# Loading later, more scratch buffers and spread spatial products in the projection phase of a hybrid decoder step

## The chip, the cores and the metric

The kernel runs on one core of one Trainium2 chip. The metric is the device time of one execution in microseconds (us), the median of several runs. The engines are called PE (TensorE, the matmuls), PEld (its weight loads, which overlap with PE), DVE (VectorE), ACT (ScalarE), POOL (GpSimd) and SP (SyncE, which here issues almost all DMAs).

## The reference

One layer of a hybrid decoder, for a prompt of 2048 tokens (16 blocks of 128 rows) and for 64 rows of a sample batch (8 sequences of 8 tokens, with 1024 cached tokens each). Cut to what matters here:

```python
def project(x, pos, norm_g, w_in, qn_g, kn_g, ln_g, ln_b, w_s, b_s):
    h = rmsnorm(x, norm_g)
    z = h @ w_in                                   # 1024 -> 3656 columns
    q, k, v, qi, ki, wi, ga, u, vm, gm = jnp.split(z, offs, axis=-1)
    ...                                            # RMSNorm and partial rotary on q, k; rotary on qi, ki
    vn = layernorm(jax.nn.gelu(vm), ln_g, ln_b)
    s = chunk_spatial_gate(vn, w_s, b_s)           # per group g: tril(w_s[g]) @ vn of each 128-row chunk
    gm_out = jax.nn.gelu(u) * s * jax.nn.silu(gm)

def indexer_scores(qi, wi, ki):
    dots = jnp.einsum('bthd,bld->bthl', qi, ki)
    return jnp.einsum('bth,bthl->btl', wi, jax.nn.relu(dots))

# per block of 128 queries: the 256 best causal keys by indexer score (top-k),
# attention over those keys only, output times silu(ga); then concat with gm_out,
# output projection, residual, and a gated per-layer embedding.
```

The sample rows do the same with keys from a paged cache, which are found through `page_table`.

## The kernel before

A class `Builder` writes the whole program: `phase_a` projects, scores and selects; `phase_b` attends; `phase_c` does the output side. The change lies in `phase_a` alone.

`phase_a` takes the blocks in three rounds (`ROUNDS`): blocks 0 to 4 and the sample block (SB), then 5 to 10, then 11 to 15. In each round it goes over 14 column chunks of `w_in` (`CH`), in the order x1 (indexer key, head weights and half of the indexer queries, 328 columns), x2 (the other half of the queries), vm0, vm1, k, v, u0, u1, gm0, gm1, q0, q1, ga0, ga1 (256 columns each). A chunk's weights are split into a rounded high part `whi` and a remainder `wlo`. In round 0, `load_w` (L265) brings them as eight `raw` tiles (L281) from a pool of six buffers, POOL or ACT writes `whi` (L287 on POOL), DVE writes `wlo` (L288), and `keep_w` (L291, its DMAs L293) writes both back to DRAM, so that rounds 1 and 2 load them ready. There are two `whi` and two `wlo` tiles: the weights of the next chunk are asked for at the start of the current one.

`proj` (L305) does a block's matmuls: `whi` and `wlo` with `hhi` (L318, L319), then `whi` with `hlo` (L321); for the sample block L311, L312 and an evacuation through `vt` (L314 on ACT, L315 on DVE). Their result `z` has two PSUM buffers. `hhi` and `hlo` are the transposed, split inputs (PE L249, ACT L123, DVE L124). `post` (L346) treats `z` by the chunk's name. For x1 it copies the indexer key to `kin` (ACT L357, a tile with two buffers), rotates it (DVE L132 to L135), sends it to the output (SP L361, `idx_k_prompt<-kin`) and transposes it into `ki_stack` (PE L365, ACT L367, DVE L368); the queries go as `qn` to the DRAM scratch `s_qi` (L378, L381). For vm1 the LayerNorm is `vst` (L423 to L425), then `vn` times and plus `lng` on POOL (L429, L430). `spatial` (L331) is the mixing product of one group for all blocks of the round: PE L337 (prompt blocks) and L342 (sample), out through ACT L338 and L343 into the `vn` tile, with two `tp` PSUM buffers shared with all transposes. In round 0 the eight groups are called from chunk k's block 3 on and through chunk v.

Beside the projections runs the indexer. After each block's `post` the function `pump` is called with a budget and draws steps from generators: `idx` (the queries are loaded by `load_qi` L652 and transposed L666, then dots on PE L681/L682, relu on ACT L684, weighted sum on DVE L686), `sample_idx` for the sample block (its keys come by indirect DMA on POOL, L695, with the row numbers `prow` that `page_rows` computes on DVE, L189 and L190), and `topk` (a search for the threshold, ACT L822 with short DVE steps, then full-width DVE passes). After round 2 the last part of `phase_a` computes the gMLP half of the output projection (`gm` products: PE L560 transposes, L572, L573, L576 matmuls) while the last top-ks run, and prepares the keys of phase B (PE L1014, ACT L1016, DVE L1017).

The order in which the code is written is a priority; a scheduler at build time fixes the order of instructions on each engine and of DMAs on SP. On the chip each engine then works strictly in that order.

Of the kernel before, what the change touches and what calls it, by code (L numbers as in the profile page):

```python
# [9 lines left out]
F32 = mybir.dt.float32  # L10
# [13 lines left out]
SB = 16  # L24
# [17 lines left out]
FILL_AT = 4  # L42
LAG_SM = 4
# [67 lines left out]
class Builder:  # L111
# [85 lines left out]
    def phase_a(self, eb):  # L197
        tc, nc, I, O = self.tc, self.nc, self.I, self.O
        with ExitStack() as es:
# [13 lines left out]
            rp = pool("a_raw", 6)  # L213
# [131 lines left out]
            def post(name, b, z):  # L345
# [3 lines left out]
                if name == "x1":  # L349
                    w = z[:, 64:72]  # L350
                    if b == SB:
                        nc.vector.tensor_scalar(self.absw[:P, b], w, rs, (8 * 64) ** -0.5, op0=OP.mult, op1=OP.mult)
                    else:
                        nc.scalar.activation(self.absw[:P, b], w, AF.Abs, scale=self.rs2[:P, b:b + 1])
                        nc.scalar.activation(self.sgn[:P, b], w, AF.Sign)
                    kin2 = wk.tile([128, 2, 64], F32, name="kin")[:P]
                    nc.scalar.activation(kin2, z[:, None, 0:64].to_broadcast([P, 2, 64]), AF.Copy, scale=rs)  # L357
                    self.rope(nc.vector, kin2, rt, 2, wk, P)
                    kin = kin2[:, 0]
                    dst = O["idx_k_sample"].rearrange("o a t d -> (o a t) d") if b == SB else O["idx_k_prompt"][0, 0, b * 128:(b + 1) * 128]  # L360
                    nc.sync.dma_start(dst, kin)  # L361

                    def ki_t():
                        ps = self.tp.tile([128, 4, 128], F32, name="tp")
                        nc.tensor.transpose(ps[:, 0, :P], kin2.rearrange("p a d -> p (a d)"), ident[:P, :P])  # L365
                        kst = self.ki[:, b, :P]
                        nc.scalar.activation(kst, ps[:, 0, :P], AF.Copy)  # L367
                        nc.vector.tensor_tensor(kst[64:128], ps[64:128, 0, :P], kst[64:128].bitcast(F32), OP.subtract)  # L368

                    later.append(ki_t)  # L370
# [76 lines left out]
            primed, active = [], [None]  # L447
# [3 lines left out]
            def pump(budget):  # L451
                credit[0] = min(credit[0], 0.0) + budget
                while credit[0] > 0 and (blocks_due or primed or dots or tops):
                    if not primed and blocks_due and not (dots and active[0] == SB):
# [3 lines left out]
                    if not dots and primed and len(tops) < 2:  # L458
                        active[0], g = primed.pop()
                        dots.append(g)  # L460
                    turn[0] ^= 1
                    l = (dots, tops)[turn[0]]
                    if l:
                        try:
                            v = next(l[0])
                            if isinstance(v, tuple):
                                tops.append(self.topk(*v))
                                v = 0
                            credit[0] -= v
                        except StopIteration:  # L470
# [16 lines left out]
            for si, (r, c) in enumerate(seq):  # L487
# [9 lines left out]
                nxt = load_w(seq[si + 1][1], seq[si + 1][0]) if si + 1 < len(seq) else None  # L497
                if si == 0:
# [4 lines left out]
                    lng = ac.tile([128, 2, 512], F32, name="lng")  # L503
                    nc.sync.dma_start(lng[:, 0], bcast(I["ln_v_g"], 512))
                    nc.sync.dma_start(lng[:, 1], bcast(I["ln_v_b"], 512))
# [10 lines left out]
                    self.io8 = io8  # L516
                    self.cnew = tk.tile([64, 64], F32, name="cnew")
# [3 lines left out]
                if not nxt:  # L521
                    ws = [load_out(0)]
                for j, b in enumerate(blocks):
                    z = proj(cur, b)
                    for f in later:
                        f()
                    later.clear()
                    post(name, b, z)
                    n, s = 2 * len(blocks) - 2, {"k": j - 2, "v": len(blocks) - 2 + j}.get(name, -1)
                    if s >= 0:  # L530
                        for g in range(8 * s // n, 8 * (s + 1) // n):
                            spatial(blocks, g)
# [1047 lines left out]
```

## Time and profile before

| | us |
|---|---|
| median of 3 runs | 1902.33 |
| the three runs | 1901.91, 1902.33, 1904.38 |
| the profiled execution | 1904.02 |
| its span (first to last instruction) | 1902.2 |
| PE busy in the span | 1835.5 (96%) |
| DVE busy | 1244.3 (65%) |
| ACT busy | 1018.8 (54%) |
| POOL busy | 631.2 (33%) |
| DMA traffic | 261.54 MB, mean 137 GB/s |

PE's share is the first number to read: what PE does not work, or works at half clock, is all that an edit of order can win in the stretches in which it is the bound. A row of waits reads: engine, tile and line that waited, the engine, tile and line waited for, the total in us, how often, and the longest.

### The profile page before, as it was taken

Reading aid. Unit: us, or ns where it says so; the run is one execution under the profiler, and the core shown is the slowest. Engines: PE = TensorE matmul, PEld = TensorE weight load, DVE = VectorE, ACT = ScalarE, POOL = GpSimd, SP = SyncE. Lnnn points to the kernel's source line nnn. Section 1 sums busy time; section 2 is a strip of 40 time slices with the busy share of each in tenths; the row PEclk is TensorE's granted clock in tenths of the full one; section 3 lists DMA queues with packets and bytes.
Section 4 is the critical chain, followed back from the end, with each engine's and each line's share of the span. In section 5 each row is a group of like instructions: output and inputs, shape, how many; then the busy total and the mean of one; then the engine's idle time right before and its main releaser. Section 6 shows DMA issues by size and latency. Waiting matters only on the chain. (4 is left out here: it accounts for less than half of the span.)

```text
span 1902.2 us, 33981 instructions
## 1 busy us (share of the span) xinstructions
PE 1835.5 (96%) x11974; PEld 1602.0 (84%) x11974; DVE 1244.3 (65%) x3631; ACT 1018.8 (54%) x1909; POOL 631.2 (33%) x950
## 2 busy tenths in 40 slices
PE   7989998999999999999989899999999999999998
PEld 6889978999999999999867678777787777888887
DVE  4497655458778638778752789888998765223321
ACT  4245434346666636667654788877888653122221
POOL 4483463324003324004403443232221374222221
PEclk9989999999999999999999899999999999999999
DMA  8655656544445564454463432233220373222211
GB/s 285 200 163 180 207 188 210 186 131 147 127 155 169 202 188 141 151 164 166 139 206 130 134 102 87 66 100 95 67 67 23 98 246 130 75 96 99 98 36 45
DMA packets 243807, 261.54 MB, mean 137 GB/s; under 512 B 83176, under 2 KB 209840, under 8 KB 243248
## 3 DMA queue, kind: packets, MB, share of 16 engines
q1 hardware_dynamic: 237744, 240.45, 40.0%
q0 software_dynamic: 5888, 18.88, 3.3%
q8 instruction: 95, 1.56, 0.3%
q14 instruction: 80, 0.66, 0.1%
HBM read 171.90 MB, written 87.37 MB: 136 GB/s over the span
## 5 line engine op out<-in xcount | busy, mean ns | idle before, releaser
L318 PE MATMUL z<-whi,hhi 128*128 128x256 f32 (+1 forms) x1792 | 461.2, 292 | 11.3 <-ACT qn L392 3.9
L319 PE MATMUL z<-wlo,hhi 128*128 128x256 f32 (+1 forms) x1792 | 453.1, 287 | 0.2 <-DVE wlo L288 0.2
L318 PEld LDWEIGHTS z<-whi,hhi 128*128 128x128 f32 x1792 | 341.0, 190 | 22.1 <-ACT qn L392 4.3
L319 PEld LDWEIGHTS z<-wlo,hhi 128*128 128x128 f32 x1792 | 340.9, 190 | 5.7 <-DVE wlo L288 1.5
L321 PE MATMUL z<-whi,hlo 128*128 128x256 f32 (+1 forms) x1792 | 264.4, 286 | 0.0
L321 PEld LDWEIGHTS z<-whi,hlo 128*128 128x128 f32 x1792 | 238.4, 190 | 2.4
L686 DVE SCALAR_TENSOR_TENSOR big<-dots,sgn,big 128x1024 f32<-128x1024 f32 (+7 forms) x176 | 179.2, 1018 | 62.3 <-ACT dots L684 58.2
L124 DVE TENSOR_TENSOR b_pt<-b_tp,b_pt 128x512 fp32r<-128x512 f32 (+1 forms) x288 | 183.3, 655 | 11.8 <-ACT b_pt L123 10.5
L684 ACT ACTIVATE dots<-dots 128x1024 f32<-128x1024 f32 (+7 forms) x176 | 140.7, 802 | 93.0 <-PE dots L682 88.1
L1148 PE MATMUL b_o<-b_pt,Vst 128*128 128x512 f32 x544 | 183.7, 423 | 0.9 <-DVE b_pt L124 0.8
L123 ACT ACTIVATE b_pt<-b_tp 128x512 fp32r<-128x512 f32 (+1 forms) x288 | 155.5, 577 | 49.4 <-PE b_tp L1131 44.2
L1131 PE MATMUL b_tp<-mats,b_sm 128*128 128x128 f32 x1088 | 171.9, 275 | 3.1 <-DVE b_pt L124 1.8
L822 ACT ACTIVATE bfw<-big,tk 128x384 bf16<-128x384 f32 (+14 forms) x105 | 136.4, 1299 | 52.6 <-DVE tk L842 38.1
L1105 ACT ACTIVATE b_sm<-b_sm,b_st 128x128 f32<-128x128 f32 (+15 forms) x128 | 154.8, 1210 | 15.7 <-DVE b_st L1098 14.6
L1131 PEld LDWEIGHTS b_tp<-mats,b_sm 128*128 128x128 f32 x1088 | 131.5, 141 | 34.9 <-ACT b_sm L1105 4.9
L1096 PE MATMUL b_s<-Kst,b_qh 128*128 128x512 f32 (+3 forms) x320 | 139.5, 439 | 6.9 <-DVE b_st L1098 4.3
L1098 DVE CUSTOM_DVE_ANT_0 b_sm<-b_s,b_mask,b_st 128x512 f32<-128x512 f32 (+3 forms) x192 | 123.9, 646 | 24.8 <-PE b_s L1097 17.3
L1097 PE MATMUL b_s<-Kst,b_ql 128*128 128x512 f32 (+3 forms) x320 | 117.4, 369 | 0.0
L681 PE MATMUL dots<-ki_stack,qih 128*128 128x512 f32 (+3 forms) x304 | 112.7, 372 | 1.6 <-DVE big L686 1.6
L1464 PE MATMUL c_mm<-c_l_w_ple_gate,c_mh 128*128 128x512 f32 x272 | 107.1, 394 | 2.6 <-DVE c_l_w_ple_gate L1417 2.6
L682 PE MATMUL dots<-ki_stack,qil 128*128 128x512 f32 (+3 forms) x304 | 109.6, 369 | 0.0
L1463 PE MATMUL c_mm<-c_h_w_ple_gate,c_mh 128*128 128x512 f32 x272 | 109.3, 402 | 0.0
(351 smaller groups left out, 3758.4 us busy)
## 6 DMA issues: line engine op xcount, KB each, us to landing
whi<-s_wh SPq DMA_DIRECT2D x52, 512.0 KB
wlo<-s_wl SPq DMA_DIRECT2D x52, 512.0 KB
raw<-w_in SPq DMA_DIRECT2D x112, 128.0 KB
s_wh<-whi SPq DMA_DIRECT2D x13, 1024.0 KB
s_wl<-wlo SPq DMA_DIRECT2D x13, 1024.0 KB
s_r<-hlo SPq DMA_DIRECT2D x32, 256.0 KB
b_qr<-s_q SPq DMA_DIRECT2D x32, 256.0 KB
c_r<-s_r SPq DMA_DIRECT2D x16, 512.0 KB
```

The lines of the kernel that those rows point to most:

```text
L123: nc.scalar.activation(hi, src, AF.Copy)
L124: nc.vector.tensor_tensor(lo, src, hi.bitcast(F32), OP.subtract)
L318: nc.tensor.matmul(z, lhsT=hh[:, k], rhs=wh[:, k, :n], start=(k == 0), stop=False)
L319: nc.tensor.matmul(z, lhsT=hh[:, k], rhs=wl[:, k, :n], start=False, stop=False)
L321: nc.tensor.matmul(z, lhsT=hl[:, k], rhs=wh[:, k, :n], start=False, stop=(k == 7))
L684: nc.scalar.activation(r, r, AF.Relu)
L686: nc.vector.scalar_tensor_tensor(a, r, self.sgn[:, b, h:h + 1], a, op0=OP.mult, op1=OP.add)
L822: nc.scalar.activation(junk, acc[:P], AF.Sign, bias=cur[:, 0:1], accum_out=cur[:, 1:2])
L1096: nc.tensor.matmul(ps, lhsT=qh[:, h], rhs=rhs, start=True, stop=False)
L1105: nc.scalar.activation(part, part, AF.Exp, bias=stt[:, h, c:c + 1], scale=-1.0, accum_out=stt[:, h, 4 + e:5 + e])
L1131: nc.tensor.transpose(ps[:, k, r], sm2[r][:, (k0 + k) * 128:(k0 + k) * 128 + 128], ident)
L1148: nc.tensor.matmul(o.rearrange("p a b -> p (a b)"), lhsT=Vst[:, kb, g].rearrange("p a d -> p (a d)"), rhs=pt[:, k].rearrange("p a b -> p ( ...
```

## The change

Six things change, all in `phase_a`. The `kin` tile has four buffers (KIN) where it had the two of its pool, and the `raw` pool five where it had six. `pump` asks for the queries of the next indexer block only after four dots steps of the current one, and, when no dots are left, puts the top-k that has just done a step at the end of the list, so that two top-ks would go in turns. The constants that were loaded in the first chunk (x1) are divided: the small matrices, `guess`, the query and key norms and two index rows go to chunk x2, the LayerNorm rows `lng`, `cnew` and `page_rows` to chunk vm0. The weights of the next chunk are asked for after the first block's projection (round 0) or the second's (rounds 1 and 2). The spatial products are called one per block: four on the last blocks of chunk v and four on the first blocks of u0.

```diff
@@ -40,6 +40,7 @@
 FILL = 128
 PV_YIELD = 1
 FILL_AT = 4
+KIN = 4
 LAG_SM = 4
 LEAD = 2
 SPS = 0
@@ -210,7 +211,7 @@
             self.wk2 = right("a_wk2", 1)
             hp = pool("a_h", 6)
             wp = pool("a_w", 2)
-            rp = pool("a_raw", 6)
+            rp = pool("a_raw", 5)
             xp = ei.enter_context(tc.tile_pool(name="a_x", bufs=2, reuse_waits="tile"))
             self.big = big
             self.dp = pool("a_dots", 2, space=PSUM)
@@ -353,7 +354,7 @@
                     else:
                         nc.scalar.activation(self.absw[:P, b], w, AF.Abs, scale=self.rs2[:P, b:b + 1])
                         nc.scalar.activation(self.sgn[:P, b], w, AF.Sign)
-                    kin2 = wk.tile([128, 2, 64], F32, name="kin")[:P]
+                    kin2 = wk.tile([128, 2, 64], F32, name="kin", bufs=KIN)[:P]
                     nc.scalar.activation(kin2, z[:, None, 0:64].to_broadcast([P, 2, 64]), AF.Copy, scale=rs)
                     self.rope(nc.vector, kin2, rt, 2, wk, P)
                     kin = kin2[:, 0]
@@ -444,29 +445,33 @@
             self.idx_rate = 0
             blocks_due, dots, tops = [], [], []
 
-            primed, active = [], [None]
+            primed, active, steps = [], [None], [0]
 
             credit, turn = [0.0], [0]
 
             def pump(budget):
                 credit[0] = min(credit[0], 0.0) + budget
                 while credit[0] > 0 and (blocks_due or primed or dots or tops):
-                    if not primed and blocks_due and not (dots and active[0] == SB):
+                    if not primed and blocks_due and not (dots and (active[0] == SB or steps[0] < 4)):
                         b = blocks_due.pop(0)
                         primed.append((b, self.sample_idx() if b == SB else self.idx(b)))
                         next(primed[0][1])
                     if not dots and primed and len(tops) < 2:
                         active[0], g = primed.pop()
+                        steps[0] = 0
                         dots.append(g)
                     turn[0] ^= 1
                     l = (dots, tops)[turn[0]]
                     if l:
                         try:
                             v = next(l[0])
+                            steps[0] += l is dots
                             if isinstance(v, tuple):
                                 tops.append(self.topk(*v))
                                 v = 0
                             credit[0] -= v
+                            if l is tops and not (dots or primed or blocks_due):
+                                tops.append(tops.pop(0))
                         except StopIteration:
                             l.pop(0)
 
@@ -494,15 +499,11 @@
                         vslot[b] = (t, j)
                 if si == 2:
                     self.gmlp_weights(ac)
-                nxt = load_w(seq[si + 1][1], seq[si + 1][0]) if si + 1 < len(seq) else None
-                if si == 0:
+                if si == 1:
                     self.more_mats()
                     guess = tk.tile([128, 17, 3], F32, name="guess")
                     nc.sync.dma_start(guess, I["c_guess"])
                     self.guess = guess
-                    lng = ac.tile([128, 2, 512], F32, name="lng")
-                    nc.sync.dma_start(lng[:, 0], bcast(I["ln_v_g"], 512))
-                    nc.sync.dma_start(lng[:, 1], bcast(I["ln_v_b"], 512))
                     self.qkg = qkg = ac.tile([128, 2, 64], F32, name="qkg")
                     nc.sync.dma_start(qkg[:, 0], bcast(I["q_norm_g"], 64))
                     nc.sync.dma_start(qkg[:, 1], bcast(I["k_norm_g"], 64))
@@ -514,22 +515,28 @@
                     nc.gpsimd.iota(io8, pattern=[[1, 8]], base=0, channel_multiplier=0,
                                    allow_small_or_imprecise_dtypes=True)
                     self.io8 = io8
+                if si == 2:
+                    lng = ac.tile([128, 2, 512], F32, name="lng")
+                    nc.sync.dma_start(lng[:, 0], bcast(I["ln_v_g"], 512))
+                    nc.sync.dma_start(lng[:, 1], bcast(I["ln_v_b"], 512))
                     self.cnew = tk.tile([64, 64], F32, name="cnew")
                     nc.sync.dma_start(self.cnew, I["c_new"][:64])
 
                     self.page_rows()
-                if not nxt:
-                    ws = [load_out(0)]
                 for j, b in enumerate(blocks):
                     z = proj(cur, b)
+                    if j == (1 if r else 0):
+                        if si + 1 < len(seq):
+                            nxt = load_w(seq[si + 1][1], seq[si + 1][0])
+                        else:
+                            ws = [load_out(0)]
                     for f in later:
                         f()
                     later.clear()
                     post(name, b, z)
-                    n, s = 2 * len(blocks) - 2, {"k": j - 2, "v": len(blocks) - 2 + j}.get(name, -1)
-                    if s >= 0:
-                        for g in range(8 * s // n, 8 * (s + 1) // n):
-                            spatial(blocks, g)
+                    g = {"v": j + 4 - len(blocks), "u0": 4 + j if j < 4 else -1}.get(name, -1)
+                    if g >= 0:
+                        spatial(blocks, g)
                     if name == "ga1":
                         if j < len(nb):
                             load_x(nb[j])
```

What this does to the order of instructions is seen in three places. Line numbers in the changed kernel are 1 to 7 higher.

On SP at the start of the program, just behind the loads of x (`big<-x_prompt`): the weights of x2 (`raw`), the writes of x1's weights (`s_wh`, `s_wl`), constants and x1's first results. Before:

```order
L281 DMA raw<-w_in 128x256 x6
L154 DMA mats<-c_mats 128x256
L501 DMA guess<-c_guess 128x51
L504 DMA lng<-ln_v_g 128x512
L505 DMA lng<-ln_v_b 128x512
L507 DMA qkg<-q_norm_g 128x64
L508 DMA qkg<-k_norm_g 128x64
L518 DMA cnew<-c_new 64x64
L179 DMA pt<-page_table 128x64
L361 DMA idx_k_prompt<-kin 128x64
L281 DMA raw<-w_in 128x256
L381 DMA s_qi_72<-qn 128x256
```

and now:

```order
L282 DMA raw<-w_in 128x256 x5
L294 DMA s_wh_225<-whi 128x2624
L294 DMA s_wl_226<-wlo 128x2624
L155 DMA mats<-c_mats 128x256
L505 DMA guess<-c_guess 128x51
L362 DMA idx_k_prompt<-kin 128x64
L382 DMA s_qi_72<-qn 128x256
L508 DMA qkg<-q_norm_g 128x64
L509 DMA qkg<-k_norm_g 128x64
L626 DMA big<-w_s 128x8x128
L520 DMA lng<-ln_v_g 128x512
L282 DMA raw<-w_in 128x256
```

The two writes of x1's kept weights, which stood behind all eight `raw` loads of x2, now stand ahead of the last three of them, together with the spatial weights (`w_s`) and one half of `lng`. The page table (`pt`) and `cnew` have gone behind the `raw` loads. The first indexer key goes out with fewer constants ahead of it.

On PE in round 0, chunk k, between the projections of block 4 (L321, `z_1909`; now L322, `z_1903`) and of the sample block (L311; now L312). `dots_1956` and `dots_1944` belong to block 3's indexer, `dots_2185` to block 4's, whose queries are `qih_2084`. Before:

```order
L321 MATMUL z_1909<-whi_1340,hlo_392 128x256 x8
L681 MATMUL dots_1956<-ki_stack_221,qih_1470 128x512
L682 MATMUL dots_1956<-ki_stack_221,qil_1471 128x512
L337 MATMUL tp_1898<-vn_1008,wsT_1009 128x320
L342 MATMUL tp_1901<-vn_1008,wsS_1010 64x64
L337 MATMUL tp_1950<-vn_1008,wsT_1009 128x320
L311 MATMUL z_1961<-whi_1340,hhi_412 128x256
```

and now:

```order
L322 MATMUL z_1903<-whi_1365,hlo_392 128x256 x8
L688 MATMUL dots_1944<-ki_stack_221,qih_1464 128x512
L689 MATMUL dots_1944<-ki_stack_221,qil_1465 128x512
L338 MATMUL tp_2164<-vn_984,wsT_985 128x320
L688 MATMUL dots_2185<-ki_stack_221,qih_2084 128x512
L689 MATMUL dots_2185<-ki_stack_221,qil_2085 128x512
L688 MATMUL dots_2185<-ki_stack_221,qih_2084 128x128
L689 MATMUL dots_2185<-ki_stack_221,qil_2085 128x128
L343 MATMUL tp_2167<-vn_984,wsS_986 64x64
L338 MATMUL tp_2220<-vn_984,wsT_985 128x320
L312 MATMUL z_1949<-whi_1365,hhi_412 128x256
```

The first spatial products still stand in chunk k, at the same place; but four dots matmuls of the next indexer block now stand between the first and the second group, and the first sample product is behind them.

On PE behind round 2, at the last dots of the last indexer block (`dots_11964`); z_12758 is one gm product of twelve matmuls. Before:

```order
L572 MATMUL z_12758<-whi_12346,hhi_12726 128x512
L573 MATMUL z_12758<-wlo_12347,hhi_12726 128x512
L576 MATMUL z_12758<-whi_12346,hhi_12726 128x512 x4
L560 MATMUL tp_12924<-mats_60,hlo_12868 128x128 x4
L681 MATMUL dots_11964<-ki_stack_221,qih_11513 128x512
L682 MATMUL dots_11964<-ki_stack_221,qil_11514 128x512
```

and now:

```order
L583 MATMUL z_12734<-whi_12399,hhi_12718 128x512 x4
L688 MATMUL dots_11964<-ki_stack_221,qih_11513 128x512
L689 MATMUL dots_11964<-ki_stack_221,qil_11514 128x512
L567 MATMUL tp_12924<-mats_60,hlo_12868 128x128 x4
L579 MATMUL z_12758<-whi_12399,hhi_12726 128x512
L580 MATMUL z_12758<-wlo_12400,hhi_12726 128x512
```

The last dots stand ahead of the gm product `z_12758` and not behind it; the rows that follow, up to the first L1014 (now L1021) that has `tp_13059`, are ten gm products before and eleven now.

## Rows read from the trace of the kernel before

**Rows 1.** The page's first part: busy time of each engine, its share of the span and the number of instructions.

```profile
PE 1835.5 (96%) x11974; PEld 1602.0 (84%) x11974; DVE 1244.3 (65%) x3631; ACT 1018.8 (54%) x1909; POOL 631.2 (33%) x950
```

**Rows 2.** Busy time by stretches: the stretch in us and its length, then busy us and instructions of PE, PEld, DVE, ACT and POOL, the mean granted clock of PE (1.00 is 2.4 GHz), the DMA engines' busy share and GB/s.

```profile
25.00:50.00 25.00, 17.78 (x104) 15.86 (x103) 13.37 (x45) 8.74 (x25) 13.84 (x34) 0.86 0.88 315
50.00:75.00 25.00, 22.48 (x174) 21.73 (x175) 11.65 (x36) 3.41 (x9) 14.46 (x39) 0.93 0.75 220
...
125.00:150.00 25.00, 19.90 (x116) 16.73 (x117) 22.81 (x87) 9.79 (x24) 21.41 (x26) 0.80 0.55 172
...
275.00:300.00 25.00, 22.22 (x148) 19.17 (x149) 16.20 (x54) 8.42 (x21) 14.08 (x20) 0.93 0.49 154
...
375.00:975.00 600.00, 599.54 (x4407) 569.81 (x4406) 438.58 (x1424) 365.30 (x583) 154.70 (x245) 1.00 0.50 160
975.00:1000.00 25.00, 16.16 (x75) 13.19 (x73) 14.23 (x67) 14.15 (x21) 1.87 (x4) 0.89 0.49 161
```

**Rows 3.** The waits of PE from 25 to 75 us (chunks x1 and x2 of round 0): who waited, for whom, us in total, times, longest.

```profile
PE z L318 <- DVE kin L134: 2.5, 1, 2.5
PE tp L249 <- DVE hlo L124: 2.4, 2, 1.5
PE z L318 <- DVE vt L315: 1.7, 1, 1.7
PE z L318 <- DVE qn L378: 1.4, 1, 1.4
PE z L311 <- DVE kin L134: 1.1, 1, 1.1
```

**Rows 4.** Busy time by stretches of 5 us, columns as in rows 2.

```profile
35.00:40.00 5.00, 2.99 (x14) 2.10 (x15) 2.96 (x10) 2.62 (x10) 4.11 (x10) 0.55 1.07 357
40.00:45.00 5.00, 4.46 (x23) 4.18 (x22) 0.29 (x3) 0.72 (x4) 0.65 (x3) 0.77 1.07 372
...
55.00:60.00 5.00, 4.40 (x24) 4.43 (x25) 2.78 (x12) 0.76 (x2) 4.40 (x14) 0.66 0.83 219
```

**Rows 5.** Waits of ACT, of DVE and of POOL from 15 to 60 us, columns as in rows 3.

```profile
ACT kin L357 <- DMA idx_k_prompt<-kin: 11.6, 2, 6.0
...
DVE prow L190 <- DMA pt<-page_table: 1.5, 1, 1.5
...
POOL whi L287 <- DMA raw<-w_in: 3.0, 2, 2.5
```

**Rows 6.** The timeline of the same stretch, from several engines: start and duration in us, engine, line, operation, output and inputs, count, and in brackets the idle time before with what ended it.

```profile
26.69 0.38 SPq L281 DMA_DIRECT2D raw<-w_in  x1
27.55 0.33 SPq L293 DMA_DIRECT2D s_wh<-whi  x1
...
31.78 0.26 DVE L190 TENSOR_SCALAR prow<-pt,off 32x16 int32<-32x16 int32 x1
31.97 0.67 DVE L124 TENSOR_TENSOR hlo<-tp,hhi 128x512 fp32r<-128x512 f32 x1
...
38.49 0.37 SPq L361 DMA_DIRECT2D idx_k_prompt<-kin  x1
...
44.28 0.37 ACT L357 ACTIVATE kin<-z,rs 128x128 f32<-128x128 f32 x1 [6.05 <-DMA idx_k_prompt<-kin]
...
50.01 0.36 PE L318 MATMUL z<-whi,hhi 128*128 128x256 f32 x1 [1.72 <-DVE vt L315]
50.91 0.37 SPq L361 DMA_DIRECT2D idx_k_prompt<-kin  x1
...
54.46 0.37 ACT L357 ACTIVATE kin<-z,rs 128x128 f32<-128x128 f32 x1 [5.54 <-DMA idx_k_prompt<-kin]
```

**Rows 7.** The list of DMA issues: tensors, queue, operation, count, KB each.

```profile
s_wh<-whi SPq DMA_DIRECT2D x1, 1312.0 KB
s_wl<-wlo SPq DMA_DIRECT2D x1, 1312.0 KB
```

**Rows 8.** The waits of PE from 120 to 150 us (chunk k of round 0), columns as in rows 3.

```profile
PE tp L337 <- POOL vn L430: 2.1, 1, 2.1
PE tp L337 <- ACT vn L338: 1.8, 1, 1.8
PE dots L681 <- DVE big L686: 1.6, 2, 0.9
PE tp L342 <- POOL vn L430: 0.3, 1, 0.3
```

**Rows 9.** The timeline of POOL and PE in that stretch, columns as in rows 6.

```profile
128.12 1.19 POOL L390 TENSOR_TENSOR qst<-qst,half 128x4 f32<-128x4 f32 x1
129.28 1.66 POOL L429 TENSOR_TENSOR vn<-vn,lng 64x512 f32<-64x512 f32 x1
...
130.91 1.25 POOL L430 TENSOR_TENSOR vn<-vn,lng 128x512 f32<-128x512 f32 x1
132.22 1.44 PE L337 MATMUL tp<-vn,wsT 128*128 128x320 f32 x2 [2.14 <-POOL vn L430]
```

**Rows 10.** The timeline of DVE and PE behind the last dots, columns as in rows 6.

```profile
960.68 0.74 DVE L686 SCALAR_TENSOR_TENSOR big<-dots,sgn,big 128x512 f32<-128x512 f32 x1
...
985.56 1.07 PE L576 MATMUL z<-whi,hhi 128*128 128x512 f32 x4
...
988.28 1.07 PE L576 MATMUL z<-whi,hhi 128*128 128x512 f32 x4
998.18 1.11 PE L1014 MATMUL tp<-mats,b_kd 128*128 128x128 f32 x4 [8.84 <-DVE Kst L1017]
...
997.43 1.30 DVE L1017 TENSOR_TENSOR Kst<-tp,Kst 64x512 fp32r<-64x512 f32 x2
```

**Rows 11.** The waits of PE over the whole span, the third of the list.

```profile
PE z L318 <- ACT qn L392: 3.9, 2, 2.7
```

## The prediction

> **What bounds the kernel now.** The page's first part comes first: PE is busy 1835.5 of the 1902.2 us span, 96% [rows 1]. So only what PE idles, or does at the lower clock, can be won, some 67 us in all, and the busy shares of the other engines say nothing by themselves. The second view is busy time by stretches, to find where PE idles [rows 2]. From 375 to 975 us it is busy 599.54 of 600 at full clock: there is nothing to win there, and what is saved before arrives whole at the end, since nothing in that stretch gives way to another bound. The losses that the change can reach lie in three places: chunks x1 and x2 of round 0 (25 to 75 us, 7.22 + 2.52 = 9.7 us idle), chunk k of round 0 (125 to 150 us, 5.1 idle), and the end of phase A (975 to 1000 us, 8.84 idle). The third view is what PE waits for in each of these, and the fourth the timeline around those waits. The profiled execution took 1904.02 us, 1.7 above the median of the runs, and the sum below is made against it.
>
> **x1 and x2 (first place).** PE's waits here are 2.5 + 1.7 + 1.1 us behind the indexer keys and the sample block's evacuation, 2.4 for `hlo` and 1.4 for `qn` [rows 3]. Behind them stand two chains.
>
> The first is the key buffer. ACT waits 11.6 us in two times for the DMA that sends `kin` out [rows 5]: the copy of block 3 could start only at 44.28, 5.8 us after SP issued the DMA at 38.49, and that of block 4 at 54.46, after an issue at 50.91 [rows 6]. With four tiles, block 4's copy waits for block 0's DMA and block 3's for nothing. PE gets its `z` buffers back earlier: of the 2.5, 1.7 and 1.1 us I count 4.5 of 5.3 as gone. The rest stays because after ACT the rotation on DVE still comes before the queries are read out of `z`.
>
> The second is DVE's queue. The page rows wait 1.5 us for the page table [rows 5] and then hold DVE between other work until after 33 us; the `hlo` for which PE waits begins at 31.97, right behind one of them [rows 6]. In the new order `pt` is asked for behind the `raw` loads and the rows are computed in chunk vm0. I take the 2.4 us for `hlo` as gone, less 0.8 that remains since `hlo` also waits for ACT's rounding, and half of the 1.4 for `qn`: 2.3.
>
> The clock comes on top. It was granted at 0.55 from 35 to 40 us, 0.77 from 40 to 45 and 0.66 from 55 to 60, each time behind waits [rows 4]; that is between its two levels, 1.2 and 2.4 GHz. Over 25 to 75 us the means 0.86 and 0.93 [rows 2] say that 2 x 0.14 x 25 = 7 and 2 x 0.07 x 25 = 3.5 us passed at the lower level, which loses at most half of it, 5.25 us. With about six tenths of the waits gone I count as much of it back, 3.2.
>
> Against this: the `raw` pool of five. In round 0 POOL waits for a raw load 3.0 us at most [rows 5] and PE hardly feels it; 0 to 3.0, taken at 0.5, near the bottom, since there is no row in which PE waits for a weight DMA. And the DMAs that now stand ahead of x2's last loads, with the queries asked for later: no row of before has that wait. It can cost 0, as the loads were issued by 26.69 and not used before 50.01 [rows 6], or up to the 6.0 us of one DMA's round trip [rows 5]; I take 1.0, because the loads had 23 us to spare. Sum of the first place: 4.5 + 2.3 + 3.2 - 1.5 = 8.5, from 2 (only `hlo`, no clock) to 14 (nearly all of the 9.7 + 5.25).
>
> **Chunk k (second place).** PE waits 2.1 and 0.3 us for the LayerNorm's last step on POOL, 1.8 for ACT to empty a spatial product, and 1.6 for the dots' sum on DVE [rows 8]. The call of the spatial products is moved by a chunk, yet in the new order the first one still stands right behind block 4's projection. What changes is POOL's order: the last prompt block's L430, at 130.91, had the 1.19 us of an L390 and the 1.66 of the sample's L429 ahead of it [rows 9], and both now come behind. That is 2.85 against a wait of 2.14, so I count the 2.1 + 0.3 as gone. Between first and second group there are now four dots matmuls, so half of the 1.8 goes, 0.9. The 1.6 stays: those dots have the same neighbours. The clock of 0.80 over 25 us is 2 x 0.2 x 25 = 10 us at the lower level, but with 5.1 of these idle only some 5 us of work went at half speed, so 2.5 lost at most; 1.2 back. Sum: 2.4 + 0.9 + 1.2 = 4.5. The upper end is 9 (5.1 idle, 2.5 clock, and 1.4 for the even spacing). The lower end is a loss of 3: the hoisted dots need the next block's queries, which were asked for after four steps, and a PE that waits in order for them pays in the size of the waits here, 2.1 and 0.9 long.
>
> **End of phase A (third place).** PE stands 8.84 us before an L1014 whose buffer DVE frees at 997.43 + 1.3 [rows 10]: the L1017 ahead of it is queued on DVE behind the last top-k, which starts with the last dots' sum at 960.68. The chain from there is 36.8 us long and the change does not shorten it. In the new order one gm product more stands behind the last dots. One takes 988.28 - 985.56 = 2.72 us [rows 10], and the work is only moved, so the top-k starts that much earlier against PE: 2.7, from 0 to 5 (the clock of 0.89 in that stretch [rows 2] would give a little too).
>
> **What I cost at nothing.** The turns of the top-ks: in the order of ACT and DVE no two top-ks alternate after the change either; the last two still run one after the other, so the condition hardly ever holds with two in the list. PE's 3.9 us of waits for `qn` L392 [rows 11], near 275 to 300 us where the clock is 0.93 [rows 2]: the instructions there stand in the order of before. Rounds 1 and 2 ask for weights one block later, hidden as long as PE is the bound, since those rows have no wait for weights. Phases B and C keep their order but for a few transposes; 2 us either way.
>
> **Sum.** 8.5 + 4.5 + 2.7 = 15.7; 1904.0 - 15.7 = 1888.3, and less the 1.7 to the median's scale 1886.6: I say 1887.
>
> **Rivals.** *The start is bound elsewhere.* The DMA engines were 88% busy at 315 GB/s from 25 to 50 us and full in the 5 us stretches [rows 2, 4]; if the `kin` DMAs only shared a crowded queue, the wait moves from ACT to the sample evacuation or the raws. Then only places two and three count, less 1 us: 1902.3 - 6.2 = 1896.
>
> *x2's weights come late (slower).* The two writes of 1312 KB [rows 7], 2.69 MB, now go ahead of x2's last three loads; at the 315 GB/s of that stretch they take 8.5 us, the 0.79 MB of `w_s` and half of `lng` (by their shapes in the order) another 2.5. Ready loads at about 27.5 become 38.5 with their splits at 39 to 41. That costs nothing while PE finishes x1 later than this; PE came to x2 at 50.01 [rows 6]. It decides if the last load lands after 50: the five-buffer pool and the SP queue (the loads stand behind the first key and query, which wait for their engines) would have to add another 10 us. Then x2 starts some 3 us later than before, the queries written in x2 come back late by one trip of 6.0 [rows 5] in place two, which gains nothing; less the 2.7 of place three: 1902.3 + 3 + 6 - 2.7 = 1908.6. The Trainium skill speaks for this one: DMA: Bandwidth & Descriptors, section "Queues, rings and completion order", says that SP's DMAs go through one ring on each DMA engine and that descriptors are consumed in ring order, so a small load cannot pass the big writes; by that alone the loads come the 8.5 us later worked out above, and the sum stands only as the slack is larger. Before, the writes at 27.55 followed the last load at 26.69 [rows 6], so no run here has shown it.
>
> *Spatial products wait as before.* POOL is busy 21.41 of the 25 us here [rows 2], and if it falls behind by the 2.85 us that its order gave back, the 2.1 and 1.8 return and place two gives nothing: 1886.6 + 4.5 = 1891.
>
> *Nothing comes of it.* The start's gains are eaten in chunks that follow (75 to 150 us, where DVE is at 22.81 of 25 [rows 2]), and only the end's 2.7 or less remains: 1901.
>
> **How the numbers follow.** Forecast 0.48, spatial products as before 0.18, start bound elsewhere 0.16, nothing 0.08, weights late 0.10. About 0.2%, 3.8 us, is what a measurement of this kernel can tell from no change: faster is below 1898.5, slower above 1906.1. Faster: the first two, and three quarters of the third with its own spread, 0.78; same: 0.12; slower: 0.10. The range reaches from 1877 (the upper ends of places one and two together, 5.5 + 4.5 better) to 1900; it holds the forecast and two rivals, and leaves out the slow one and most of "nothing".
>
> **What would show it.** Right: ACT's wait for `idx_k_prompt` gone and x2 starting some 7 us earlier than 50.01; clock 1.00 in most of 25 to 60 us; no PE wait for POOL at the first L338; PE's last wait before L1021 near 6 us. Wrong: PE waiting for `whi` or `wlo` at x2's start, for `qih` in chunk vm0 to k, or DVE and POOL as the bound through 150 us with the same idle sum.

## The result and the profile after

The changed kernel takes 1892.87 us (median of 5 runs, 1890.36 to 1895.01) where the kernel before had 1902.33; the ratio is 0.9943 [0.9927, 0.9958]. That is 9.5 us less, where 15.3 were forecast. The profiled execution took 1893.5 us with a span of 1891.7, 10.5 shorter than before.

Busy time of the changed kernel, answering to [rows 1]:

```profile
PE 1833.5 (97%) x11974; PEld 1601.0 (85%) x11974; DVE 1242.1 (66%) x3631; ACT 1018.2 (54%) x1909; POOL 623.5 (33%) x950
```

The work is the same; the span is shorter because PE idles less. Its busy time by stretches, columns as in [rows 2] (stretches late in the program are moved by 10 us to meet the same work):

```profile
25.00:50.00 25.00, 21.44 (x139) 20.42 (x136) 17.04 (x60) 10.58 (x32) 15.14 (x41) 0.86 0.79 246
50.00:75.00 25.00, 23.51 (x183) 22.49 (x182) 11.02 (x26) 4.81 (x9) 14.10 (x37) 0.93 0.90 276
...
125.00:150.00 25.00, 20.74 (x126) 18.58 (x127) 20.72 (x95) 11.01 (x27) 15.33 (x23) 0.80 0.55 171
...
275.00:300.00 25.00, 25.00 (x199) 23.30 (x198) 16.04 (x62) 8.25 (x20) 11.52 (x17) 1.00 0.54 166
300.00:325.00 25.00, 20.04 (x156) 19.63 (x155) 10.91 (x61) 15.54 (x31) 2.88 (x7) 0.93 0.72 242
325.00:350.00 25.00, 25.00 (x182) 24.93 (x181) 13.76 (x45) 12.90 (x36) 9.33 (x29) 1.00 0.67 216
...
375.00:965.00 590.00, 587.59 (x4306) 557.54 (x4305) 438.06 (x1423) 364.34 (x581) 148.75 (x232) 1.00 0.50 159
965.00:990.00 25.00, 18.24 (x82) 14.83 (x81) 14.93 (x65) 14.29 (x21) 1.78 (x4) 0.89 0.54 170
```

From 300 to 350 us the kernel before had:

```profile
300.00:325.00 25.00, 24.58 (x202) 23.72 (x202) 12.85 (x66) 11.44 (x22) 6.53 (x11) 1.00 0.83 274
325.00:350.00 25.00, 21.55 (x164) 20.80 (x162) 14.87 (x56) 16.25 (x34) 8.42 (x22) 1.00 0.69 226
```

From 25 to 50 us PE gained 3.7 us of work, but the clock is the 0.86 of before; 125 to 150 is hardly better; 275 to 300 is now full and at full clock, which the forecast did not count. From 300 to 325 PE idles more than before, and the mean clock of 0.93 that stood at 275 to 300 is now here; 325 to 350 idles less. The long middle, which idled 0.5 us, now idles 2.4. PE's waits over the whole span, columns as in [rows 3]:

```profile
PE tp L1021 <- DVE Kst L1024: 7.3, 2, 6.2
PE tp L250 <- DMA x<-x_prompt: 5.9, 1, 5.9
PE z L319 <- ACT vt L414: 5.0, 2, 2.5
PE tp L567 <- DVE Kst L1024: 3.4, 3, 1.8
PE dots L688 <- DVE mk L833: 3.1, 1, 3.1
PE z L319 <- DVE vt L316: 2.7, 1, 2.7
PE z L319 <- ACT qn L393: 2.2, 2, 1.9
...
PE z L579 <- ACT hhi L124: 1.3, 1, 1.3
...
PE tp L338 <- ACT vn L339: 1.1, 1, 1.1
...
PE tp L338 <- POOL vn L431: 0.5, 1, 0.5
```

How far the changed kernel is ahead can be read point by point: the products of `proj` with `hlo` (L321 before, L322 now) come eight to a block in the same count, so the start of the last one of a chunk before, less the start of the same one in another run, is the time saved up to there. The last two columns take the first score of phase B (L1096) and the difference of spans.

| us saved at the end of | x1 | x2 | gm0 | q1 | x1, round 1 | x1, round 2 | phase B starts | span |
|---|---|---|---|---|---|---|---|---|
| time before | 44.1 | 70.6 | 219.2 | 294.0 | 364.1 | 667.9 | 1054.0 | 1902.2 |
| changed | 6.9 | 3.7 | 5.6 | 11.4 | 11.3 | 9.0 | 8.9 | 10.5 |
| e1 | -0.1 | 3.3 | 6.3 | 11.8 | 14.2 | 12.2 | 17.5 | 18.5 |
| e2 | 6.4 | 3.3 | 5.5 | 11.0 | 14.1 | 14.2 | 12.2 | 14.5 |
| e3 | 6.2 | 3.6 | 6.0 | 11.5 | 14.7 | 10.7 | 10.9 | 11.4 |
| e4 | 6.8 | 4.1 | 5.3 | 10.8 | 12.4 | 9.7 | 7.0 | 7.1 |
| e5 | -2.7 | 1.6 | 1.7 | 7.2 | 10.1 | 10.2 | 8.9 | 8.7 |
| e6 | 5.9 | 4.0 | 6.1 | 11.6 | 14.0 | 14.1 | 12.3 | 14.3 |
| e7 | 2.2 | 3.5 | 4.3 | 4.0 | 4.5 | 4.5 | 5.1 | 6.9 |
| e8 | -0.5 | -1.0 | 0.9 | 0.4 | 0.5 | -3.3 | -1.9 | 0.3 |
| e9 | 0.6 | 1.5 | 2.1 | 5.8 | 5.6 | 5.7 | 5.9 | 8.9 |
| e10 | 2.5 | 1.7 | 1.7 | 7.9 | 9.7 | 9.8 | 9.3 | 10.2 |
| e11 | 7.1 | 4.0 | 4.7 | 10.2 | 12.2 | 12.3 | 18.7 | 16.1 |
| e12 | 1.2 | 0.7 | 1.1 | 6.6 | 8.7 | 8.8 | 21.4 | 23.9 |

Of the changed kernel's 10.5 us, 5.6 come up to the end of gm0 and 5.8 from there to q1; 2.3 are lost in round 1, and what the end of phase A gains it gives back. The last 1.6 come in phases B and C, where the granted clock of the kernel before fell once (a mean of 0.93 from 1565 to 1590 us) and that of the changed kernel did not. The table is of one profiled execution each, which for e9 was the fastest of its runs and for e4 and e11 the slowest; how much a kernel is worth is said by the timed ratios below. (One of e7's twelve runs took 6284 us; its ratio leaves that run out.)

### The profile page after: what moved, and what is told of

The parts are those of the page before. It is cut to its first block, busy times and chain, and to the rows that moved or that the text cites. A ratio compares the mean times of both kernels' runs of the same rounds, so it can differ in the third digit from the quotient of the medians.

```text
span 1891.7 us, 33962 instructions
## 1 busy us (share of the span) xinstructions
PE 1833.5 (97%) x11974; PEld 1601.0 (85%) x11974; DVE 1242.1 (66%) x3631; ACT 1018.2 (54%) x1909; POOL 623.5 (33%) x950
## 4 chain that ended last, share of the span: by engine, by line
PE 83%; DVE 5%; DMA 5%; POOL 2%; issue 2%; ACT 2%; SPq 0%; DVEq 0%; POOLq 0%; ACTq 0%
PE z L319 10%; PE z L320 10%; PE z L322 10%; PE b_o L1155 7%; PE b_tp L1138 6%; PE c_mm L1471 5%; PE c_mm L1470 5%; PE c_mm L1474 5%; PE b_s L1103 3%; PE dots L688 3%; PE dots L689 3%; PE b_s L1104 3%; PE z L579 1%; PE z L580 1%; PE z L583 1%
## 5 line engine op out<-in xcount | busy, mean ns | idle before, releaser
L319 PE MATMUL z<-whi,hhi 128*128 128x256 f32 (+1 forms) x1792 | 463.0, 292 | 10.5 <-ACT vt L414 5.0
L322 PE MATMUL z<-whi,hlo 128*128 128x256 f32 (+1 forms) x1792 | 262.6, 286 | 0.0
L322 PEld LDWEIGHTS z<-whi,hlo 128*128 128x128 f32 x1792 | 237.7, 190 | 2.0
```

The source lines that it names most:

```text
L319: nc.tensor.matmul(z, lhsT=hh[:, k], rhs=wh[:, k, :n], start=(k == 0), stop=False)
L322: nc.tensor.matmul(z, lhsT=hl[:, k], rhs=wh[:, k, :n], start=False, stop=(k == 7))
```

## The experiments

My theory before the runs was that the key buffers carry the start, and the place of the spatial products the gain in q0 and q1; the rivals were the constants and the later queries. Four runs take one edit out of the changed kernel.

**e1**, two key buffers again:

```diff
-KIN = 4
+KIN = 2
```

> The changed kernel with two kin buffers in place of four; all else as changed. Theory A (the key buffers carry the start): ACT's two waits for the key DMAs come back, some 10 us in all, PE ends x1 of round 0 about 5 to 6 us later than the changed kernel (near 43 us, against 37.2), and most of the 4.6 us that the changed kernel has won by the end of vm0 is gone: about 1896 to 1897. Theory B (the constants that left the start carry it): x1 ends within 2 us of the changed kernel, the time is within 1.5 us of 1892.9.

Measured: 1886.98 us, ratio to before 0.9918 [0.9900, 0.9935]. Both theories miss. ACT waits for the key DMAs again (4.7 us, not the 10 of theory A) and x1 ends 7 us later, as A says; but at the end of x2 only 0.4 us is left of that difference, at gm0 nothing, and the whole is rather faster than the changed kernel (whose interval it just meets). PE's waits behind the keys are back:

```profile
PE z L319 <- DVE qn L379: 2.5, 1, 2.5
PE z L319 <- DVE kin L135: 2.5, 1, 2.5
```

**e2**, the spatial products as before (the old two lines on `n, s` and the loop over `g` in place of the new ones):

```diff
-                    g = {"v": j + 4 - len(blocks), "u0": 4 + j if j < 4 else -1}.get(name, -1)
-                    if g >= 0:
-                        spatial(blocks, g)
+                    n, s = 2 * len(blocks) - 2, {"k": j - 2, "v": len(blocks) - 2 + j}.get(name, -1)
+                    if s >= 0:
+                        for g in range(8 * s // n, 8 * (s + 1) // n):
+                            spatial(blocks, g)
```

> The changed kernel with the spatial products called through chunks k and v as before. Theory A (chunk k's gain is POOL's order, and the 5.5 us won in chunks q0 and q1 come from where the spatial products and the dots behind them stand): q0 and q1 of round 0 lose the 5.5 us again, chunk k to gm0 loses about 1: about 1898 to 1900. Theory B (the gain in q0 and q1 comes from the later asking for queries): the gain there stays, the time is 1893 to 1895.

Measured: 1891.98 us, 0.9939 [0.9922, 0.9955]. q0 and q1 of round 0 keep the gain, so A falls there; and from round 1 on nothing is lost any more (14.1 at its start, 14.2 in round 2), where the changed kernel loses 2.3.

**e3**, constants and page rows in x1 again (the block of `if si == 1` and `if si == 2` back under `if si == 0`):

```diff
-                if si == 1:
+                if si == 0:
...
-                if si == 2:
```

> The changed kernel with all constants and the page rows in chunk x1, as before. Theory A (key buffers carry the start): x1 ends up to 2.4 us later, as DVE works on the page rows ahead of hlo, and 1.5 to 2.5 us are lost: about 1895. Theory B (constants carry it): x1 ends 5 us later, about 1897 to 1898. Against both: nothing lost, as SP's place for lng and cnew costs x2 the same.

Measured: 1894.59 us, 0.9957 [0.9943, 0.9971]; x1 ends 0.7 us later. The third answer: beside the other edits no worth of the constants shows, as the two intervals overlap.

**e4**, queries asked for at once:

```diff
-                    if not primed and blocks_due and not (dots and (active[0] == SB or steps[0] < 4)):
+                    if not primed and blocks_due and not (dots and active[0] == SB):
```

(The counter `steps` goes with it.)

> The changed kernel with pump as before but for the inert rotation: the next block's queries are asked for at once. If the queries carry the gain in q0 and q1: 5 us lost there, about 1898. If the spatial products do: within 1.5 us of 1892.9, and the gain in q0 and q1 stays.

Measured: 1891.6 us, 0.9935 [0.9919, 0.9952]: nothing hangs on the queries, the gain in q0 and q1 stays. So no single edit that was taken out carries it. All four kept three edits. Two of them, the turns of the top-ks and the later asking for weights, change nothing in this kernel: without either, the instructions of all engines stand in the same order. The third is the smaller `raw` pool, the edit that the prediction had booked as a cost. The next four make one edit in the kernel before (e6 two, as four key buffers don't fit beside six raw ones).

**e5**, five raw buffers alone; **e6**, with four key buffers too:

```diff
+KIN = 4
...
-            rp = pool("a_raw", 6)
+            rp = pool("a_raw", 5)
...
-                    kin2 = wk.tile([128, 2, 64], F32, name="kin")[:P]
+                    kin2 = wk.tile([128, 2, 64], F32, name="kin", bufs=KIN)[:P]
```

> The kernel before with only the raw pool cut from six to five, nothing else. Theory C (the 5.5 us in chunks q0 and q1 of round 0 come with any change that moves SP's weight loads or the sample's indexer against the chunk, five raw buffers among them): q1 ends 4 us or more earlier than before, 1896 to 1899. Theory D (they need the key buffers, the constants or the spatial products moved as well): q1 as before, 1902 to 1904 on the scale on which before is 1902.3.

> The kernel before with four kin buffers and five raw ones, nothing else. The prediction's first place alone: 4.5 us of waits and part of the clock won in x1, 5 us or more at the end of x1. Theory E (DVE's queue through chunks k and v takes back what the start wins beyond 5 to 6 us, whatever wins it): the gain at the end of gm0 is 4 to 6 us as in all kernels so far. If the constants are needed for it, under 3 there.

Measured: e5 1895.75 us, 0.9967 [0.9956, 0.9979]; e6 1890.51 us, 0.9941 [0.9925, 0.9956]. Theory C holds for these buffers: five raw ones alone win the 5.5 us (from 1.7 at gm0 to 7.2 at q1) and 2.9 more up to round 1. (Not any change does it, as C has it: e7 and e8 below gain nothing from gm0 to q1.) And these two edits together are as fast as the whole change. Where the 5.5 come from shows on POOL at the turn from q0 to q1. The kernel before:

```profile
272.26 5.69 POOL L287 TENSOR_SCALAR whi<-raw,gk 128x256 fp32r<-128x256 f32 x7
278.04 0.24 POOL L389 TENSOR_SCALAR qst<-qst 64x4 f32<-64x4 f32 x1
...
278.94 1.01 POOL L390 TENSOR_TENSOR qst<-qst,half 64x4 f32<-64x4 f32 x1
```

and with five raw buffers (e5):

```profile
266.19 3.13 POOL L287 TENSOR_SCALAR whi<-raw,gk 128x256 fp32r<-128x256 f32 x5 [1.23 <-PE z L311]
269.58 1.00 POOL L287 TENSOR_SCALAR whi<-raw,gk 128x256 fp32r<-128x256 f32 x1 [0.27 <-DMA raw<-w_in]
270.66 0.64 POOL L389 TENSOR_SCALAR qst<-qst 64x4 f32<-64x4 f32 x1
271.38 1.01 POOL L390 TENSOR_TENSOR qst<-qst,half 64x4 f32<-64x4 f32 x1
```

When q0's last block frees the weight tile, POOL splits all tiles that lie ready, seven before, and the sample block's norm (`qst`) stands behind them in POOL's order. From there it goes on through `qn` (three buffers), the DMA to `s_q`, ACT's copy and the `z` buffer to PE, in the kernel before:

```profile
289.50 0.47 ACT L392 ACTIVATE qn<-z,rs 128x256 f32<-128x256 f32 x1 [5.01 <-DMA s_q<-qn]
290.02 0.39 PE L318 MATMUL z<-whi,hhi 128*128 128x256 f32 x1 [2.73 <-ACT qn L392]
```

That is the longer of the two waits of [rows 11]. The other ended at 269.05, before the row of seven began at 272.26, so the row can't be its cause. Ahead of the norm on which it hangs, POOL had two of the sample indexer's indirect DMAs:

```profile
262.27 1.09 POOL L695 DMA_INDIRECT sraw<-cache_idx_k,prow  x1 [0.28 <-POOL qid L747]
263.67 0.96 POOL L695 DMA_INDIRECT sraw<-cache_idx_k,prow  x1 [0.30 <-issue]
264.70 0.19 POOL L389 TENSOR_SCALAR qst<-qst 128x4 f32<-128x4 f32 x1
```

With five raw buffers these two stand further ahead, and PE has neither wait:

```profile
254.42 1.10 POOL L695 DMA_INDIRECT sraw<-cache_idx_k,prow  x1 [0.28 <-POOL qid L747]
255.82 0.96 POOL L695 DMA_INDIRECT sraw<-cache_idx_k,prow  x1 [0.30 <-issue]
```

**e7**, the constants alone (the two blocks of the change); **e8**, the spatial products alone (e2's diff the other way):

> The kernel before with only the constants and the page rows moved to chunks x2 and vm0. Theory E: x1 ends about 2 us earlier, and 2 to 5 us are won at the end of gm0, so that the constants alone do much of what the key buffers do. Against it: under 1 us at gm0.

> The kernel before with only the spatial products moved to chunks v and u0. The prediction's second place: 4.5 us won between the end of vm1 and gm0. Theory F, from the kernel that lacks only this edit: it wins 1 us or less there and costs 2 to 3 us in chunks q0 and q1 of round 1, where a wait of PE for qn appears: no gain, 1901 to 1905 on the scale on which before is 1902.3, unless q0 and q1 of round 0 win their 5.5 us.

Measured: e7 1898.77 us, 0.9979 [0.9969, 0.9989]; e8 1902.47 us, 0.9996 [0.9985, 1.0008]. The constants alone win 4.3 us at gm0, the key buffers with five raws 6.1, all together 5.6: the gains of the start do not add up (theory E). The spatial products win nothing: 1.9 us between x2 and gm0, and 3.8 are lost in round 1, where PE waits for `qn` a third time (5.7 us in three waits against the 3.9 in two of [rows 11]) and the granted clock behind that wait falls to a mean of 0.83 from 595 to 605 us:

```profile
PE z L318 <- ACT qn L392: 5.7, 3, 2.7
```

**e9** and **e10** test the row of splits itself:

```diff
-                    if ci == 0 and k % 2:
+                    if ci in (0, 12) and k % 2:
```

> The kernel before, six raw buffers, with only this: of the eight high-half weight splits of chunk ga0 in round 0, four go to ACT in place of POOL. Theory G (five raw buffers win the 5.5 us of q0 and q1 because POOL then splits five and not seven tiles in a row, 5.69 us, ahead of the norm of the queries): that stretch of POOL falls to some 3 us and q1 of round 0 ends 4 to 5.5 us earlier than before, about 1897 to 1898 on the scale on which before is 1902.3. Rival H (the order of SP's loads wins it): q1 gains under 1 us, 1902.

```diff
-            rp = pool("a_raw", 6)
+            rp = pool("a_raw", 4)
```

> The kernel before with four raw buffers, nothing else. Theory G: q1 of round 0 gains 5 us or more, as with five, since the row of splits is as short or shorter; the start loses up to 3 us more than with five: 1895 to 1899. Rival H (the order of SP's loads): no reason for the gain to stay; 1899 to 1904.

Measured: e9 1897.96 us, 0.9986 [0.9977, 0.9995]; e10 1895.09 us, 0.9973 [0.9961, 0.9985]. In e9 POOL splits three tiles in a row, and the norm is no longer behind seven:

```profile
269.59 1.68 POOL L287 TENSOR_SCALAR whi<-raw,gk 128x256 fp32r<-128x256 f32 x3
274.18 0.48 POOL L287 TENSOR_SCALAR whi<-raw,gk 128x256 fp32r<-128x256 f32 x1 [2.91 <-DMA raw<-w_in]
275.59 0.30 POOL L389 TENSOR_SCALAR qst<-qst 64x4 f32<-64x4 f32 x1 [0.93 <-DVE qst L388]
```

q1 wins 3.7 us (2.1 to 5.8) with PE's order unchanged, the 2.7 us wait for `qn` is gone, and 0.5 and 1.3 us of waits remain just ahead of it. So theory G holds for some two thirds of the 5.5, and e10 fits it; rival H, with under 1 us, falls. The rest is as large as the two waits that remain (3.7 + 0.5 + 1.3 = 5.5), and e5 and e10 have neither: the 0.5 is for `qn`, behind the indirect DMAs, which e9 leaves in their place, and the 1.3 for the sample block's evacuation on DVE. The 2.9 of e5 at the turn to round 1 stand against three waits of the kernel before, 1.7 us for the load of `x`, 1.0 for `hlo` and 0.5 for `sgn`; e5 has none of them and e9 1.3, 1.0 and 0.5. Why they go is not shown. The timed gain of e9 (2.6 us) is smaller than expected.

**e11** and **e12** look for a faster kernel, at PE's wait for the K transposes, which stays in all of them and is 11.2 us in e2. Both have the spatial products of e2, and besides:

```diff
-EARLY = 15
+EARLY = 18
```

> The changed kernel with the spatial products as before (the run e2) and phase B's key preparation begun three gm products later (EARLY 18 for 15). 14 gm products in place of 10 stand between the last dots and the K transposes that wait for DVE, 10.9 us of work against the wait of 11.2: that wait falls under 2 us, of which three more K transposes at the end of phase A give back 2 to 5: 1884 to 1888 where e2 had 1892.0, the fastest so far but for e1, or faster. If the wait only moves to the end of the phase: within 2 us of e2.

> The run e11 with two kin buffers in place of four. Theory A (the key buffers carry the start): PE ends x1 6 to 7 us later and 4 us or more are left of that at the start of round 1: 1887 to 1890. Theory E, as e1 suggests (what x1 wins is given back by the end of chunk v of round 0): x1 ends 6 to 7 us later, but at the start of round 1 the two are within 2 us of each other: 1882 to 1885.

Measured: e11 1883.46 us, 0.9912 [0.9899, 0.9926]; e12 (with `KIN = 2`) 1881.05 us, 0.9887 [0.9868, 0.9905], both faster than the changed kernel. The wait for the K transposes in e2 and then in e11:

```profile
PE tp L1022 <- DVE Kst L1025: 12.2, 2, 11.2
```

```profile
PE tp L1022 <- DVE Kst L1025: 3.0, 2, 1.9
```

The wait went as expected, with gm products standing where PE was idle; e11 gains 6.4 us from round 2 to phase B where e2 loses 2. In e12 the key buffers do show at the start of round 1 (8.7 against 12.2), against theory E, yet it ends no slower. What four key buffers are worth at the end is open, as its sign changes: beside five raw ones in the kernel before they help (e6 against e5), in the changed kernel two do rather better (e1), and two do no worse in e12.

## Why the prediction was right or wrong

The direction and the range held; the point was 6 us too low. Only a part of the gain is where it was put: the three places were given 15.7 us and hold 5.6, and 5.8 came in q0 and q1, which were put at nothing. That the total still fell well inside the range is luck. Of its own signs, ACT's wait for the keys is gone and the wait before L1021 is near 6 us; x2 began at 44.19, which is 5.8 us earlier and not 7, and the clock from 25 to 60 us was not at full speed.

**The first place** was given 8.5 us; 3.7 were left at the end of x2 and 4.6 at the end of vm0. The chain of the key buffer was read rightly: ACT's waits for the key DMAs are gone and x1 ends 6.9 us earlier. The step that failed is DVE's queue, "the rows are computed in chunk vm0". They did not go that far: the page table came later, and DVE did the page rows between x1 and x2, ahead of the sample block's evacuation for which PE then waits. DVE and PE in the changed kernel:

```profile
39.85 0.51 DVE L191 TENSOR_SCALAR prow<-pt,off 64x32 int32<-64x32 int32 x2 [0.94 <-DMA pt<-page_table]
...
41.90 1.00 DVE L191 TENSOR_SCALAR prow<-pt,off 32x16 int32<-32x16 int32 x4
...
43.55 0.49 DVE L316 TENSOR_TENSOR vt<-z,vt 64x328 f32<-64x328 f32 x1
...
44.19 0.55 PE L319 MATMUL z<-whi,hhi 128*128 128x256 f32 x1 [2.75 <-DVE vt L316]
```

With that wait the clock's 3.2 us did not come back either: it is still 0.86 from 25 to 50 us and 0.93 from 50 to 75.

The page rows are not all of it. In e3, where they are back in x1, that wait is gone, and x2 ends no earlier (3.6 us saved against 3.7), since PE then waits for the transposed spatial weights (`wsT`):

```profile
PE tp L639 <- DVE wsT L631: 4.0, 1, 4.0
```

Of what x1 wins, 3.3 to 4.1 us are left at the end of x2 in all six profiled kernels with four key buffers (the changed one, e2, e3, e4, e6, e11), and e1, with two, has 3.3 there as well. So the terms of x1 could not be added up as if x2 would take nothing back; what bounds x2 is open.

**The five raw buffers**, booked at a cost of 0.5 because no row showed PE waiting for a weight DMA, are the largest win of a single edit in the kernel before (e5 0.33%, e7 0.21%, e8 0.04%; four key buffers alone can't be tried there). The pool was looked at for what it delays, and not for the row of POOL work that it lets through at once. With it fell "what I cost at nothing" for q0 and q1: "the instructions there stand in the order of before" was true of PE up to its last wait there (one pair of the sample indexer's products has moved ahead of it) and not of POOL.

**Chunk k** was given 4.5 and won 1.0 (from vm0 to gm0). The wait for POOL fell from 2.4 to 0.5 and that for ACT from 1.8 to 1.1, as forecast. But the hoisted dots wait 3.1 us for DVE, where 1.6 had been taken as unchanged: the four dots matmuls between the spatial products were counted as cover, and they are themselves bound by DVE, which is busy 20.72 of 25 us here. The sum of earlier dots ends just before they start (the row of waits names `mk`, which DVE began under it):

```profile
128.18 0.74 DVE L693 SCALAR_TENSOR_TENSOR big<-dots,sgn,big 128x512 f32<-128x512 f32 x1
128.97 0.79 PE L688 MATMUL dots<-ki_stack,qih 128*128 128x512 f32 x1 [3.06 <-DVE mk L833]
```

The clock stayed at 0.80.

**The end of phase A** was given 2.7. The wait fell by it, 8.8 to 6.2, as one more product predicts; then 0.8 more for `tp` L567 (3.4 against the 2.6 of L560), 1.0 more for `hhi` (1.3 against 0.3) and more behind it took it back: phase B starts 8.9 us ahead, where the x1 of round 2 ended 9.0 ahead. The kernel before had:

```profile
PE tp L560 <- DVE Kst L1017: 2.6, 3, 1.0
...
PE z L572 <- ACT hhi L123: 0.3, 1, 0.3
```

**"What is saved before arrives whole at the end"** failed by 2.3 us: the even spread of the spatial products costs that in round 1 (e2, e8), which was put at nothing with rounds 1 and 2. The turns of the top-ks and the later asking for weights were rightly put at nothing, as said under e4.

**The rivals.** Of "the start is bound elsewhere" the sign came, PE's wait moved to the sample evacuation, but in the changed kernel behind DVE's page rows and not behind a crowded queue. Late weights for x2 did not come about, though the loads did come later: SP issued the last three at 30.83 to 32.62, where the last had gone out at 26.69 before, as by the profile it waited for the two writes to land:

```profile
SPq L520 <- DMA s_wl<-wlo: 3.2, 1, 3.2
SPq L626 <- DMA s_wh<-whi: 1.8, 1, 1.8
```

POOL had split them by 37.84 and PE came to x2 at 44.19, so some 6 us of slack were left. As the loads went out only when the writes had landed, the runs still don't show how loads fare that are queued right behind such writes. "Spatial products wait as before" was right in its size and wrong in its cause: DVE, not POOL.

## What to carry to other kernels

Before a buffer pool is shrunk or grown, look at what its tiles let an in-order engine do in one row, and what stands behind that row: a deeper prefetch can cost more than it hides, as six raw buffers did here. A gain at the start is to be followed to the next place where another engine is the bound; two groups of edits that by themselves win 4.3 and 6.1 us up to gm0 (e7, e6) win 5.6 there together. And a moved piece of work is to be found in the new order of its own engine before its cost is counted as gone.

## What was not expected of the hardware

The split on POOL, 128x256, took 0.47 to 0.73 us in six of the row of seven, and 2.52 us in the other, over just the stretch in which DVE worked without a pause on its own splits and the norm:

```profile
274.99 2.52 POOL L287 TENSOR_SCALAR whi<-raw,gk 128x256 fp32r<-128x256 f32 x1
...
274.92 1.26 DVE L288 SCALAR_TENSOR_TENSOR wlo<-raw,gk,whi 128x256 fp32r<-128x256 f32 x3
276.11 0.40 DVE L388 TENSOR_REDUCE qst<-sq 64x4 f32<-64x256 f32 x1
276.44 0.46 DVE L288 SCALAR_TENSOR_TENSOR wlo<-raw,gk,whi 128x256 fp32r<-128x256 f32 x1
276.83 0.41 DVE L395 TENSOR_TENSOR qn<-qn,qkg 64x256 f32<-64x256 f32 x1
```

So some 2 of the 5.69 us of that row are one slow split. In e5's row of five one took 1.15 us, beside two splits on DVE in a row. Whether DVE's work holds POOL up no run takes apart.
